# RWKV-7 mixing: the next group's last inverse product, scores and transpose between the state steps, and other places for the projected block's finish, the group norm's first parts and the result copies

## The chip, the cores and the metric

The kernel runs on one core of a Trainium2 chip. Its time is the device time of one execution, in microseconds (us), and the number that stands for a kernel is the median of its runs. The kernel before has 1464.78 us, the median of three runs from 1461.38 to 1465.36.

A core has a matrix engine (TensorE, PE in the profile), a vector engine (VectorE, DVE), an activation engine (ScalarE, ACT), a general engine (GpSimd, POOL) and a queue engine that issues transfers (SyncE, SP). Each of them works through its own list of instructions in order and waits for another engine only where an instruction says so.

## The reference, cut to what matters

One decoder layer on 1024 positions: a projection `w_in`, three mixers beside each other (HGRN2, windowed attention, RWKV-7), an output projection, a gated MLP and a gated embedding. The change lies in the RWKV-7 mixer, with four heads of width 64. For each head it computes a recurrence over the positions, and a norm of every position's result over its 64 values:

```python
def step(state, inp):
    r_t, w_t, k_t, v_t, kk_t, a_t = inp
    sa = jnp.einsum('bhvk,bhk->bhv', state, -kk_t)
    state = (state * w_t[:, :, None, :] + sa[..., None] * (kk_t * a_t)[:, :, None, :]
             + v_t[..., None] * k_t[:, :, None, :])
    return state, jnp.einsum('bhvk,bhk->bhv', state, r_t)
...
_, y = lax.scan(step, s0, xs)
y = y.swapaxes(0, 1)
mean = jnp.mean(y, axis=-1, keepdims=True)
var = jnp.mean((y - mean) ** 2, axis=-1, keepdims=True)
y = ((y - mean) * lax.rsqrt(var + RK_GN_EPS)).reshape(B_, S_, RK_WIDTH) * ln_w + ln_b
```

Other columns of `w_in` feed the other two mixers. Their products are independent of the recurrence, and the kernel uses them as filling work.

## The kernel before, in words

**The recurrence in chunks.** The four heads are taken as two pairs, p = 0 and p = 1, one pair after the other; a pair fills the 128 partitions. The 1024 positions are cut into 16 chunks of 64. Inside a chunk the recurrence becomes a triangular system, whose inverse is prepared as two tables, T and U, of 32-wide blocks. Only the state S goes from chunk to chunk.

**Groups.** `rwkv_groups` takes four chunks at a time, so a pair has four groups, g = 0 to 3. In the profiled execution the groups of p 0 lie at about 146 to 216 us, those of p 1 at about 334 to 404 us. A group does the following, in this order:

- finish of an earlier projected block and parts of the norm, in some groups (below);
- the *turn* of v: two transposes on TensorE (L821), then a filling block;
- py (L860), the last product of the inverse, whose copy into SBUF on ScalarE is Y (L861), and on GpSimd the next group's score table ABt (`scores_bd`, L801);
- *place* copies on ScalarE (L828): v into XV, and after the turn of ar, ar into xr;
- the scores sc (L871), of which VectorE takes the masked AKt and W (L785), a filling block, and pu (L882) from Y and U, which VectorE copies into U (L883);
- the turn of bhat, copied by VectorE into pb (L828), then on VectorE the next group's T under its mask (`quad("T")`, L794), and on GpSimd W from pb (L888);
- the turn of khat, placed by ScalarE into W; a filling block; pk, copied by ScalarE into xr (L897); two filling blocks;
- px (L901), of which ScalarE takes half of X (L903) and XV (L905) and VectorE the other half of X (L903); two filling blocks;
- pgm (L909), to which VectorE adds the addend and writes GM (L913), and pn (L922), from which VectorE makes N; the split of a projection weight (`pending("w")`) and a filling block;
- four *state steps*, u = 0 to 3: a product pS of GM and S (L939), from which VectorE makes the next S with one instruction (L940), and the products of the result pyo (L942, L944). A filling block follows the step u = 0;
- on VectorE the next group's U under its mask (`quad("U")`, L794), on ScalarE the four copies of the result from pyo into the pair's output (L954).

The first step of group 0 needs no product, since the state before it is zero.

**Filling blocks.** `fill(1)` issues one step of a projection that is independent of the recurrence: three products of 512 columns (L130, L132, L134) into the block dp. Three projected blocks, 48 steps, are spread over a pair. A weight of a projected block is split in two parts before use: ScalarE casts (L106), GpSimd subtracts (L108). When a block is complete, `pending("z")` issues its *finish* at the next place where it is called: in p 0 two multiplies on VectorE (L470); in p 1, for the block that is complete in group 1, twice a multiply (L306), a sigmoid on ScalarE (L473) and a second multiply (L475). A store on SyncE follows.

**The norm.** The first half of a pair's result, groups 0 and 1, is normed while groups 2 and 3 run, in four parts: part 0 takes the mean off (L727 to L729, VectorE), part 1 squares (L732, ScalarE), part 2 makes the variance (L735, L736, VectorE, and a power on GpSimd), part 3 multiplies (L740, VectorE).

**What sets the order.** The groups are issued inside `manual_schedule` for TensorE, VectorE, ScalarE and GpSimd: these engines get their instructions in the order in which the code is written. SyncE's order is the scheduler's. The products' results go to a pool of four PSUM buffers, tag `mx` (py, pt, sc, pu, pk, px, pgm, pn, pyo and pS).

## Time and profile before

| | kernel before |
|---|---|
| median of three runs | 1464.78 us (1461.38 to 1465.36) |
| profiled execution | 1464.15 us |
| its span, from the first to the last instruction | 1462.4 us |
| mean granted TensorE clock | 0.994 |
| busy, of the span: PE, DVE, ACT, POOL | 98%, 75%, 44%, 31% |

All rows of the profile come from the one profiled execution. A row of the order of time has the start in us, the duration in us, the engine, the line and the operation, written as output<-inputs with the tile shapes; a bracket at the end gives the idle time before the instruction and what ended it. `x8` means that eight instructions stand in one row. A row of a table of stretches has the bounds of the stretch, its length, then for PE, weight loads, DVE, ACT and POOL the busy time with the number of instructions, and at the end the granted TensorE clock, the share of the DMA engines and GB/s.

### The profile page before, as it was taken

The page shows a single profiled execution, that of the slowest core. Times are in us where ns is not written, and L with a number is a line of the kernel's source. Part 1 is how long each engine was busy: PE and PEld are TensorE (multiplying, and loading weights), DVE is VectorE, ACT ScalarE, POOL GpSimd, SP SyncE. Part 2 cuts the span into 40 slices and gives each one's busy share as a digit, 9 for nine tenths or more (in the row PEclk, how much of TensorE's full clock was granted, in tenths as well). Part 3 has the DMA queues.
Part 4 walks back from the last instruction along what each step waited for, and adds up shares of the span by engine and source line. Part 5 has one row for each costly group of instructions (what it writes and reads, how often), then busy time and mean ns, then how long its engine had stood idle before and what let it go on. Part 6 is the DMA issues. An engine that isn't in the chain of part 4 may idle for free.

```text
span 1462.4 us, 20341 instructions
## 1 busy us (share of the span) xinstructions
PE 1431.1 (98%) x7480; PEld 1178.0 (81%) x7480; DVE 1099.2 (75%) x1672; ACT 636.1 (44%) x1131; POOL 447.8 (31%) x364
## 2 busy tenths in 40 slices
PE   9999999999999999899989999999999999999996
PEld 7888887888877777788878888888888888888885
DVE  7667565674677688638778898888898799777685
ACT  6531443213434565335544344444444444455552
POOL 3331342223321131222144554444554000002342
PEclk9999999999999999999999999999999999999998
DMA  6123021240251320265423333333233883352343
GB/s 220 63 90 105 33 71 58 65 130 30 73 188 51 108 73 30 71 219 204 156 87 105 99 100 108 102 108 106 97 107 111 309 293 95 102 172 58 123 157 116
DMA packets 80020, 167.84 MB, mean 115 GB/s; under 512 B 20081, under 2 KB 22257, under 8 KB 79921
## 3 DMA queue, kind: packets, MB, share of 16 engines
q1 hardware_dynamic: 65568, 145.44, 30.2%
q10 hardware_dynamic: 13408, 17.57, 3.6%
q0 software_dynamic: 944, 3.54, 0.7%
q8 instruction: 59, 0.97, 0.3%
q14 instruction: 41, 0.33, 0.1%
HBM read 120.12 MB, written 46.40 MB: 114 GB/s over the span
## 4 chain that ended last, share of the span: by engine, by line
PE 87%; DVE 4%; issue 3%; ACT 2%; POOL 2%; DMA 2%; SPq 0%; DVEq 0%; ACTq 0%; POOLq 0%
PE bg L1351 16%; PE bv L1351 12%; PE dp L130 8%; PE dp L134 8%; PE dp L132 8%; PE bg L1652 7%; PE bv L1652 7%; PE hsc L1029 1%; PE bv L130 1%; PE bv L132 1%; PE bv L134 1%; PE bg L130 1%; PE bg L134 1%; PE bg L132 1%; PE swq L1186 1%
## 5 line engine op out<-in xcount | busy, mean ns | idle before, releaser
L130 PE MATMUL dp<-xh,whi 128*128 128x512 f32 x544 | 197.5, 408 | 0.8 <-ACT xh L375 0.8
L134 PE MATMUL dp<-xh,wlo 128*128 128x512 f32 x544 | 188.9, 392 | 0.3 <-POOL wlo L108 0.3
L132 PE MATMUL dp<-xl,whi 128*128 128x512 f32 x544 | 188.6, 392 | 0.0
L108 POOL TENSOR_TENSOR wlo<-raw,whi 128x512 fp32r<-128x512 f32 x84 | 138.0, 1662 | 80.9 <-ACT whi L106 80.9
L108 POOL TENSOR_TENSOR wlo<-wraw,whi 128x512 fp32r<-128x512 f32 x63 | 89.2, 1420 | 226.2 <-ACT whi L106 208.2
L1351 PE MATMUL bg<-t,whi 128*128 128x512 f32 x352 | 132.7, 389 | 0.0
L106 ACT CAST whi<-wraw 128x512 fp32r<-128x512 f32 x120 | 72.6, 617 | 129.1 <-PE dp L132 87.1
L130 PEld LDWEIGHTS dp<-xh,whi 128*128 128x128 f32 x544 | 101.6, 189 | 23.6 <-issue 3.5
L134 PEld LDWEIGHTS dp<-xh,wlo 128*128 128x128 f32 x544 | 102.3, 188 | 22.5 <-POOL wlo L108 0.7
L132 PEld LDWEIGHTS dp<-xl,whi 128*128 128x128 f32 x544 | 102.5, 189 | 20.2 <-DVE xl L376 0.5
L108 POOL TENSOR_TENSOR wlo<-s,whi 128x512 fp32r<-128x512 f32 x44 | 65.7, 1492 | 159.1 <-ACT whi L106 159.1
L106 ACT CAST whi<-raw 128x512 fp32r<-128x512 f32 x88 | 52.6, 619 | 100.3 <-PE bv L1351 51.5
L1652 PE MATMUL bg<-t,whi 128*128 128x512 f32 x308 | 94.9, 389 | 0.0
L1652 PE MATMUL bv<-t,whi 128*128 128x512 f32 x308 | 94.8, 389 | 0.0
L106 ACT CAST whi<-s 128x512 fp32r<-128x512 f32 x66 | 38.9, 620 | 120.7 <-PE bg L1351 113.0
L175 POOL TENSOR_TENSOR rst<-rst,mhalf 128x4 f32<-128x4 f32 (+1 forms) x9 | 10.2, 1130 | 222.7 <-DVE rst L173 222.7
L108 DVE TENSOR_TENSOR wlo<-wraw,whi 128x512 fp32r<-128x512 f32 x57 | 47.7, 837 | 40.2 <-ACT whi L106 35.8
L1351 PEld LDWEIGHTS bg<-t,whi 128*128 128x128 f32 x352 | 66.1, 188 | 13.7
L1648 ACT CAST t<-t 128x512 fp32r<-128x512 f32 x77 | 47.8, 622 | 47.9 <-PE bv L1652 33.0
L1652 PEld LDWEIGHTS bv<-t,whi 128*128 128x128 f32 x308 | 57.8, 188 | 12.0
L1652 PEld LDWEIGHTS bg<-t,whi 128*128 128x128 f32 x308 | 57.8, 188 | 11.9
L1351 PE MATMUL bg<-t,wlo 128*128 128x512 f32 x176 | 67.2, 389 | 0.0
(424 smaller groups left out, 3616.6 us busy)
## 6 DMA issues: line engine op xcount, KB each, us to landing
raw<-in_ffn_up_dram SPq DMA_DIRECT2D x44, 512.0 KB, 3.7
wraw<-in_w_in_dram SPq DMA_DIRECT2D x29, 512.0 KB, 3.7
z<-zst SPq DMA_DIRECT2D x18, 512.0 KB, 3.0
gb<-ct SPq DMA_DIRECT2D x33, 256.0 KB, 2.3
t<-gb SPq DMA_DIRECT2D x33, 256.0 KB, 2.8
t<-gt SPq DMA_DIRECT2D x33, 256.0 KB, 2.7
zl<-z SPq DMA_DIRECT2D x16, 512.0 KB, 4.5
wraw<-in_ple_gate_dram SPq DMA_DIRECT2D x16, 512.0 KB, 3.6
```

Of the source, the lines that this page charges most:

```text
L106: nc.scalar.copy(hi, src)
L108: eng.tensor_tensor(lo, src, hi.bitcast(F32), ALU.subtract)
L130: nc.tensor.matmul(ps[hf], wh, xh[hf], start=first, stop=False)
L132: nc.tensor.matmul(ps[hf], wh, xl[hf], start=False, stop=False)
L134: nc.tensor.matmul(ps[hf], wl, xh[hf], start=False, stop=last)
L175: nc.gpsimd.tensor_tensor(r2[:, :n], r[:, :n], self.mhalf[:, :n], ALU.pow)
L1029: nc.tensor.matmul(sc[:, c, :], ks[:, c * P:(c + 1) * P], view(qt, c * P, [2 * n, 64 // n], [HT + n, 2], [1, n]), start=True, stop=True)
L1186: nc.tensor.matmul(pq[h][:, b:b + w], d["q"][hs, qb * P:nk], d["k"][hs, b:b + w], start=True, stop=True)
L1351: nc.tensor.matmul(ps, w[part == 2][:, s], X[k][part == 1], start=start and k == part == 0, stop=k == 3 and part == 2, skip_group_check=no ...
L1648: nc.scalar.copy(xh, x)
L1652: nc.tensor.matmul(ps[m], wt[part == 2][:, m * P:(m + 1) * P], (xh, xl)[part == 1], start=k == part == 0, stop=k == NK - 1 and part == 2)
```

## The change

Only `rwkv_groups` is changed; no product, copy or transfer is added or left out.

- py, its copy Y, the next group's score table and the next group's U under its mask are issued in the state steps, after the step u = 1 (`inverse_first`, then `quad("U")`). For group 0, whose U is made ahead of the loop as before, py stands ahead of the loop.
- The next group's turn of v and its filling block are issued after the step u = 2 (`values_turn`, `fill(1)`). In the last group, where nothing comes next, a filling block and norm part 3 stand after u = 1.
- The four result copies of a group are issued in the next group, after the place copies of v and ar (`result`); those of the last group behind the loop.
- `pending("z")` and, in group 2, norm part 0 move from the head of the group to behind the place of khat.
- Norm part 1 moves in group 2 from behind the place of ar to behind the copies of px; norm part 2 moves from group 2 to group 3, at the same place in the group.

There are 37 filling blocks in the groups instead of 36, and one less behind them.

```diff
+        def inverse_first(g):
+            t["Y"] = rt("Y", [P, 4, P])
+            py = mxp.tile([P, 4, P], F32, tag="mx", name=self.nm("py"))
+            for u in range(4):
+                nc.tensor.matmul(py[:, u, :], t["AB", g][:, u, :], t["T", g][:, u, :], start=True, stop=True)
+            nc.scalar.copy(t["Y"], py)
+            if g < 3:
+                scores_bd(g + 1)
+
+        def values_turn(g):
+            t["pv"] = turn(lambda b: v[:, 256 * g + P * b:256 * g + P * b + P])
+
+        def result(g, py):
...
+                    nc.scalar.copy(y4[64 * c:64 * c + 64, 2 * g:2 * g + 2, h, :], py4[64 * h:64 * h + 64, :, c, :])
+
+        S, before = None, None
+        values_turn(0)
+        fill(1)
+        inverse_first(0)
         for g in range(4):
...
-            Xr = rt("xr", [P, 4, P])
-            self.pending("z")
-            if g == 2:
-                self.rwkv_norm_in(p, d, 0, (0,))
-            if last:
-                self.rwkv_norm_in(p, d, 0, (3,))
-            pv = turn(lambda b: v[:, t2(b)])
-            fill(1)
-            Y = rt("Y", [P, 4, P])
-            py = mxp.tile([P, 4, P], F32, tag="mx", name=self.nm("py"))
...
-            place(pv, lambda h: XV[:, :, h, :], nc.scalar.copy, 1)
+            Xr, Y = rt("xr", [P, 4, P]), t["Y"]
+            place(t["pv"], lambda h: XV[:, :, h, :], nc.scalar.copy, 1)
             place(turn(lambda b: ar[:, c2(b), 0, :].rearrange("p c i -> p (c i)")), lambda h: Xr[:, :, 0:64], nc.scalar.copy)
-            if g == 2:
-                self.rwkv_norm_in(p, d, 0, (1,))
+            if before:
+                result(*before)
...
-            if g == 2:
+            if g == 3:
                 self.rwkv_norm_in(p, d, 0, (2,))
             place(turn(lambda b: d["kh"][:, t2(b)]), lambda h: W[:, :, h, 1, :], nc.scalar.copy, 1)
+            self.pending("z")
+            if g == 2:
+                self.rwkv_norm_in(p, d, 0, (0,))
             fill(1)
...
                 nc.scalar.copy(XV[q, :, h, :], px[q, :, 64:128])
+            if g == 2:
+                self.rwkv_norm_in(p, d, 0, (1,))
             fill(2)
...
                 if u == 0:
                     fill(1)
-            if not last:
-                quad("U", g + 1)
...
+                if u == 1:
+                    if last:
+                        self.rwkv_norm_in(p, d, 0, (3,))
+                        fill(1)
+                    else:
+                        inverse_first(g + 1)
+                        quad("U", g + 1)
+                if u == 2 and not last:
+                    values_turn(g + 1)
+                    fill(1)
+            before = g, py
+        result(*before)
```

**TensorE, p 1, from the end of group 1's state steps into group 2**, in the kernel before (pS and pyo are the state steps, pt a turn, dp a filling block):

```order
L939 MATMUL pS_3208<-S_3200,GM_2864 128x64
L942 MATMUL pyo_3189<-XV_2866,W_2865 64x64 x2
L944 MATMUL pyo_3189<-S_3200,GM_2864 128x64
L939 MATMUL pS_3215<-S_3207,GM_2864 128x64
L942 MATMUL pyo_3189<-XV_2866,W_2865 64x64 x2
L944 MATMUL pyo_3189<-S_3207,GM_2864 128x64
L821 MATMUL pt_3242<-cst,v_2304 128x128 x2
L130 MATMUL dp_3183<-xh_107,whi_3015 128x512
L132 MATMUL dp_3183<-xl_108,whi_3015 128x512
L134 MATMUL dp_3183<-xh_107,wlo_3017 128x512
L860 MATMUL py_3249<-T_3115,ABt_3075 128x128 x4
L821 MATMUL pt_3261<-cst,ar_2043 128x128 x2
```

The same place in the changed kernel, where L939 is L953, L942 and L944 are L956 and L958, and L860 is L849:

```order
L849 MATMUL py_3208<-T_3115,ABt_3048 128x128 x4
L953 MATMUL pS_3219<-S_3200,GM_2864 128x64
L956 MATMUL pyo_3189<-XV_2866,W_2865 64x64 x2
L958 MATMUL pyo_3189<-S_3200,GM_2864 128x64
L821 MATMUL pt_3225<-cst,v_2304 128x128 x2
L130 MATMUL dp_3183<-xh_107,whi_3015 128x512
L132 MATMUL dp_3183<-xl_108,whi_3015 128x512
L134 MATMUL dp_3183<-xh_107,wlo_3017 128x512
L953 MATMUL pS_3232<-S_3218,GM_2864 128x64
L956 MATMUL pyo_3189<-XV_2866,W_2865 64x64 x2
L958 MATMUL pyo_3189<-S_3218,GM_2864 128x64
L821 MATMUL pt_3243<-cst,ar_2043 128x128 x2
```

py now stands ahead of the third state product, the turn of v and the filling block ahead of the fourth, and the turn of ar follows directly behind the last step.

**ScalarE, p 1, group 2**, in the kernel before, from the result copies of group 1 (sc<-pyo) to the copy of pk into xr (zst is the projected block's finish, oc norm part 1):

```order
L954 COPY sc_2307<-pyo_3189 64x2x64 x4
L473 ACTIVATE zst_3228<-dp_2894 128x512 x2
L861 COPY Y_3248<-py_3249 128x512
L828 COPY XV_2866<-pt_3242 64x2x64 x4
L828 COPY xr_3227<-pt_3261 64x2x64 x4
L732 ACTIVATE oc_3237<-sc_2307 128x512
L828 COPY W_2865<-pt_3305 64x2x64 x4
L897 COPY xr_3227<-pk_3315 128x4x64
```

The same place in the changed kernel, where L861 is L850, L954 is L862, L897 is L909, L903 is L915 and L905 is L917:

```order
L850 COPY Y_3207<-py_3208 128x512
L828 COPY XV_2866<-pt_3225 64x2x64 x4
L828 COPY xr_3238<-pt_3243 64x2x64 x4
L862 COPY sc_2307<-pyo_3189 64x2x64 x4
L828 COPY W_2865<-pt_3285 64x2x64 x4
L473 ACTIVATE zst_3292<-dp_2893 128x512 x2
L909 COPY xr_3238<-pk_3309 128x4x64
L915 COPY X_2863<-px_3325 64x4x64
L917 COPY XV_2866<-px_3325 64x4x64 x2
L732 ACTIVATE oc_3301<-sc_2307 128x512
```

Y is now the first of the group's copies, the result copies stand behind the place of ar, and the two sigmoids stand between the place of khat and the copy of pk.

**VectorE, p 1, group 2**, in the kernel before, from U's mask to the copy of half of X:

```order
L794 TENSOR_TENSOR U_3221<-Tc_2510,cst 128x512
L306 TENSOR_TENSOR dp_2894<-dp_2894,rstd 128x512
L475 TENSOR_TENSOR zst_3228<-zst_3228,dp_2894 128x512
L306 TENSOR_TENSOR dp_2894<-dp_2894,rstd 128x512
L475 TENSOR_TENSOR zst_3228<-zst_3228,dp_2894 128x512
L727 TENSOR_REDUCE gnm_3238<-sc_2307 128x8
L728 TENSOR_SCALAR gnm_3238<-gnm_3238 128x8
L729 TENSOR_TENSOR sc_2307<-sc_2307,gnm_3238 128x512
L785 TENSOR_TENSOR AKt_3276<-sc_3269,pm_2858 128x256
L785 TENSOR_TENSOR W_2865<-sc_3269,pm_2858 64x4x64 x2
L883 COPY_PREDICATED U_3221<-cmask,pu_3283 128x512
L828 COPY pb_2862<-pt_3289 64x2x64 x4
```

The same engine in the changed kernel, from the masked AKt on (L883 is L892):

```order
L785 TENSOR_TENSOR AKt_3261<-sc_3254,pm_2858 128x256
L785 TENSOR_TENSOR W_2865<-sc_3254,pm_2858 64x4x64 x2
L892 COPY_PREDICATED U_3216<-cmask,pu_3268 128x512
L828 COPY pb_2862<-pt_3274 64x2x64 x4
L794 TENSOR_TENSOR T_3281<-Tc_2503,cst 128x512
L306 TENSOR_TENSOR dp_2893<-dp_2893,rstd 128x512
L475 TENSOR_TENSOR zst_3292<-zst_3292,dp_2893 128x512
L306 TENSOR_TENSOR dp_2893<-dp_2893,rstd 128x512
L475 TENSOR_TENSOR zst_3292<-zst_3292,dp_2893 128x512
L727 TENSOR_REDUCE gnm_3302<-sc_2307 128x8
L728 TENSOR_SCALAR gnm_3302<-gnm_3302 128x8
L729 TENSOR_TENSOR sc_2307<-sc_2307,gnm_3302 128x512
```

The seven instructions L306 to L729, which stood ahead of AKt, now stand behind T's mask, and the next instruction behind them is the copy of px into X (L915).

More of the change, by code (lines that the diff above doesn't have):

```diff
@@ L843, in rwkv_groups @@
         add_ar(0)
-        S = None
+        def inverse_first(g):
[9 more added lines that the diff above has]
+        def result(g, py):
+            y4 = y3.rearrange("p (b h) v -> p b h v", h=2)
+            py4 = py.rearrange("p (b two) v -> p b two v", two=2)
+            for h in (0, 1):
+                for c in (0, 1):
+                    nc.scalar.copy(y4[64 * c:64 * c + 64, 2 * g:2 * g + 2, h, :], py4[64 * h:64 * h + 64, :, c, :])
[3 more added lines that the diff above has]
+        inverse_first(0)
         for g in range(4):
@@ L848, in rwkv_groups @@
             t2 = lambda b: slice(256 * g + P * b, 256 * g + P * b + P)
-            Xr = rt("xr", [P, 4, P])
-            self.pending("z")
-            if g == 2:
-                self.rwkv_norm_in(p, d, 0, (0,))
-            if last:
-                self.rwkv_norm_in(p, d, 0, (3,))
-            pv = turn(lambda b: v[:, t2(b)])
-            fill(1)
-            Y = rt("Y", [P, 4, P])
-            py = mxp.tile([P, 4, P], F32, tag="mx", name=self.nm("py"))
-            for u in range(4):
-                nc.tensor.matmul(py[:, u, :], t["AB", g][:, u, :], t["T", g][:, u, :], start=True, stop=True)
-            nc.scalar.copy(Y, py)
-            if not last:
-                scores_bd(g + 1)
-            place(pv, lambda h: XV[:, :, h, :], nc.scalar.copy, 1)
+            Xr, Y = rt("xr", [P, 4, P]), t["Y"]
+            place(t["pv"], lambda h: XV[:, :, h, :], nc.scalar.copy, 1)
             place(turn(lambda b: ar[:, c2(b), 0, :].rearrange("p c i -> p (c i)")), lambda h: Xr[:, :, 0:64], nc.scalar.copy)
-            if g == 2:
-                self.rwkv_norm_in(p, d, 0, (1,))
+            if before:
+                result(*before)
             ps = mxp.tile([P, 4, 2, 64], F32, tag="mx", name=self.nm("sc"))
@@ L947, in rwkv_groups @@
                     fill(1)
-            if not last:
-                quad("U", g + 1)
-            y4 = y3.rearrange("p (b h) v -> p b h v", h=2)
-            py4 = py.rearrange("p (b two) v -> p b two v", two=2)
-            for h in (0, 1):
-                for c in (0, 1):
-                    nc.scalar.copy(y4[64 * c:64 * c + 64, 2 * g:2 * g + 2, h, :], py4[64 * h:64 * h + 64, :, c, :])
+                if u == 1:
[10 more added lines that the diff above has]
+        result(*before)
     def hgrn_setup(self):
```

## The prediction

> **What bounds the kernel now.** I read the page's first part and its chain of waits, then the stretches of single groups, then the order of time on TensorE, VectorE and ScalarE there.
>
> ```profile
> PE 1431.1 (98%) x7480; PEld 1178.0 (81%) x7480; DVE 1099.2 (75%) x1672; ACT 636.1 (44%) x1131; POOL 447.8 (31%) x364
> PE 87%; DVE 4%; issue 3%; ACT 2%; POOL 2%; DMA 2%; SPq 0%; DVEq 0%; ACTq 0%; POOLq 0%
> ```
>
> TensorE sets the end, and the change adds and removes no product. So it can only win time in which TensorE stands, and lose where TensorE is made to stand. The stretches below are p 1's groups 1 and 2, each from one turn of v to the next; p is the pair of heads, g the group.
>
> ```profile
> 351.08:367.92 16.84, 16.80 (x141) 14.31 (x141) 8.03 (x21) 6.23 (x21) 5.59 (x9) 1.00 0.10 32
> 367.92:386.62 18.70, 17.27 (x141) 14.26 (x141) 13.22 (x29) 10.12 (x28) 9.90 (x12) 1.00 0.07 29
> ```
>
> Group 1 is a clean group; group 2 takes 18.70 - 16.84 = 1.86 us more with the same 141 products. TensorE in time, group 1 and the first waits of group 2:
>
> ```profile
> 353.12 1.06 PE L871 MATMUL sc<-ar,kbd 128*128 128x128 f32 x8
> 355.61 0.38 PE L821 MATMUL pt<-cst,bhat 128*128 128x128 f32 x2
> 356.03 0.44 PE L821 MATMUL pt<-cst,khat 128*128 128x128 f32 x2
> 359.20 1.05 PE L901 MATMUL px<-xr,U 128*128 128x128 f32 x8
> 361.47 1.05 PE L909 MATMUL pgm<-pb,X 128*128 128x128 f32 x8
> 365.42 0.33 PE L939 MATMUL pS<-S,GM 128*128 128x64 f32 x2
> 366.21 0.39 PE L939 MATMUL pS<-S,GM 128*128 128x64 f32 x2
> 367.07 0.39 PE L939 MATMUL pS<-S,GM 128*128 128x64 f32 x2
> 367.92 0.39 PE L821 MATMUL pt<-cst,v 128*128 128x128 f32 x2
> 368.85 1.05 PE L860 MATMUL py<-T,ABt 128*128 128x128 f32 x8
> 372.49 1.16 PE L882 MATMUL pu<-U,Y 128*128 128x128 f32 x8 [0.77 <-ACT Y L861]
> 374.73 0.44 PE L821 MATMUL pt<-cst,khat 128*128 128x128 f32 x2 [0.66 <-ACT xr L828]
> ```
>
> The reader is to see three losses. In group 2, pu waits for Y and the turn of khat for ScalarE's place copies. In every group khat starts 0.42 after bhat, where its followers need about 0.2: a hidden wait of 0.20. And the chained state products lie 0.86 and 0.85 apart where the first step takes 0.79: 0.13 a group.
>
> **The change part by part.** *State steps.* The product py (L860), the turn of v and a filling block now stand between the state products, so S is ready when its product comes. I take back 0.13 in p 0's and p 1's groups 1 and 2, and 0.21 in groups 0, where three steps of 0.86 follow each other: 4 x 0.13 + 2 x 0.21 = 0.94. What a py after a state step costs beside one after a filling block no row shows; I take nothing, with 0.07 (0.86 less 0.79) either way at six places, 0.4.
>
> *Copies before khat.* Y is now copied during the state steps, so after the last step ScalarE begins with the place copies of v and ar, and stores the group's result only then.
>
> ```profile
> 368.18 1.08 ACT L954 COPY sc<-pyo 64x128 f32<-64x128 f32 x4 [6.21 <-PE pyo L944]
> 371.36 0.60 ACT L473 ACTIVATE zst<-dp 128x512 f32<-128x512 f32 x1 [1.49 <-DVE dp L306]
> 371.86 0.58 ACT L861 COPY Y<-py 128x512 f32<-128x512 f32 x1
> 372.46 1.11 ACT L828 COPY XV<-pt 64x128 f32<-64x128 f32 x4
> 373.60 1.07 ACT L828 COPY xr<-pt 64x128 f32<-64x128 f32 x4
> 376.52 0.37 ACT L897 COPY xr<-pk 128x256 f32<-128x256 f32 x1
> ```
>
> The result copy began 0.26 after the last state product (368.18 - 367.92). The score products (sc) now begin one turn, 0.22, after that step, so the v copies start at sc + 0.04, and ar is copied at 0.04 + 1.14 + 1.10 (373.60 - 372.46 = 1.14) = sc + 2.28. khat comes at sc + 2.7 (355.61 - 353.12 + 0.22): no wait. That gives 0.20 in each of groups 1 to 3 of both p, 6 x 0.20 = 1.20, and takes away the 1.86 of p 1's group 2. All gains: 0.94 + 1.20 + 1.86 = 4.00 us. The first groups' order is not changed.
>
> *Group 2: where the finish and the norm go.* The finish of the projected block (L306, L473, L475, twice) and the first norm part (L727 to L729) leave the head of group 2 and stand behind the T product mask.
>
> ```profile
> 357.67 0.69 DVE L794 TENSOR_TENSOR T<-Tc,cst 128x512 f32<-128x512 f32 x1
> 360.75 0.43 DVE L903 COPY X<-px 64x256 f32<-64x256 f32 x1 [2.39 <-ACT X L903]
> 369.91 0.69 DVE L475 TENSOR_TENSOR zst<-zst,dp 128x512 f32<-128x512 f32 x1 [0.92 <-ACT zst L473]
> 370.63 0.70 DVE L306 TENSOR_TENSOR dp<-dp,rstd 128x512 f32<-128x512 f32 x1
> 372.60 0.68 DVE L727 TENSOR_REDUCE gnm<-sc 128x8 f32<-128x512 f32 x1
> 373.31 0.17 DVE L728 TENSOR_SCALAR gnm<-gnm 128x8 f32<-128x8 f32 x1
> 373.52 0.69 DVE L729 TENSOR_TENSOR sc<-sc,gnm 128x512 f32<-128x512 f32 x1
> 374.13 0.42 DVE L785 TENSOR_TENSOR AKt<-sc,pm 128x256 f32<-128x256 f32 x1
> ```
>
> In p 1, ScalarE's two sigmoids now stand ahead of the copy of pk into xr (L897), and px (L901) needs xr. A pass of 0.69 lets the next start after 0.61 (374.13 - 373.52), so VectorE is free behind T at sc + 4.55 + 0.61 = 5.16. From there: L306 until the sigmoid starts 0.73 (371.36 - 370.63), sigmoid and handover 0.63, L475 until L306 0.72, to the second sigmoid 0.73, until ScalarE's next copy 0.50 (371.86 - 371.36), that copy 0.37, to TensorE 0.06 (373.60 + 1.07 to 374.73): 3.74, so px starts at sc + 8.90. It is due at 359.20 - 353.12 - 0.20 = sc + 5.88. **TensorE stands 3.02.** The X copy comes behind the second L475, L727, L728 and L729 at 5.16 + 3.44 + 0.61 + 0.71 + 0.21 + 0.61 = 10.74, is ready 0.43 + 0.06 later at 11.23, and pgm is due at px + 2.27 (361.47 - 359.20) = 11.17: 0.06. Together 3.08.
>
> In p 0 the finish has no sigmoid, only two multiplies (their 1.20 from the next fence): 5.16 + 1.20 + 0.71 + 0.21 + 0.61 = 7.89, X ready at 8.38; pgm is due at 5.88 + 2.27 = 8.15: 0.23.
>
> *Group 3.* The result copy (1.10 with its gap) now lies ahead of the weight cast that VectorE waits for, and the second norm part (L735, L736) ahead of the next finish and of X.
>
> ```profile
> 391.55 0.62 ACT L106 CAST whi<-wraw 128x512 fp32r<-128x512 f32 x1
> 393.42 1.20 DVE L828 COPY pb<-pt 64x128 f32<-64x128 f32 x4
> 394.94 1.29 DVE L470 TENSOR_TENSOR zst<-dp,rstd 128x512 f32<-128x512 f32 x2 [0.32 <-PE dp L134]
> ```
>
> The cast starts at sc + 2.28 + 1.10 + 0.01 = 3.39, the pb copies 1.87 after it as here (393.42 - 391.55) at 5.26, and take 1.23; the reduce 0.71, L736 0.21, the multiplies 1.20, X 0.43, the way 0.06: 9.10 against 8.15 due, so 0.95. In p 0 a sigmoid lies between ScalarE's copies of X and XV; for what it holds up I take 0.3, an estimate of half of L473's 0.60, with 0 and 0.6 as ends: 1.25. Losses: 3.08 + 0.23 + 0.95 + 1.25 = 5.51; against 4.00 that is **1.5 us slower**. Nothing else is paid: U's mask (L794) stands now between two state results, with a py of 0.89 and a v turn with its filling block of 0.93 (368.85 - 367.92) to cover its 0.69; the projected block's store on SyncE goes 5 us later and SyncE's order stays.
>
> *What a standing TensorE costs behind it.* The granted clock halves after a sparse stretch:
>
> ```profile
> 491.72:495.13 3.41, 1.63 (x13) 1.10 (x12) 1.88 (x6) 3.40 (x8) 0.00 (x0) 1.00 0.92 345
> 495.13:498.54 3.41, 3.41 (x19) 3.41 (x18) 0.09 (x1) 0.82 (x3) 0.00 (x0) 0.50 0.84 330
> 611.19:614.60 3.41, 1.87 (x13) 1.36 (x12) 1.44 (x4) 0.00 (x0) 1.01 (x1) 1.00 0.00 0
> 614.60:618.01 3.41, 3.37 (x17) 2.26 (x15) 2.61 (x3) 1.24 (x2) 1.29 (x1) 1.00 0.27 76
> ```
>
> A stretch of 3.41 with 1.78 idle is followed by one at 0.50, one with 1.54 idle by full clock. These stretches lie on a grid, since 611.19 is 35 steps of 3.413 after 491.72. A stand of 3.0 leaves more than 1.78 in one such stretch unless the grid cuts it between 1.2 and 1.8, so the drop comes in about 1 - 0.6/3.41, 0.8 of executions. It costs half of 3.41, 1.7, less what falls into the stand itself: I take 1.4, with 0 and 1.7 as ends. The Trainium skill (TensorE: Matmul & The Clock Gate, HAM oscillation — how this bites in real kernels) gives the rule "no PE-idle gaps >~3.4µs", by which a stand of 3.0 keeps the clock and the sum stays at 1.5; the rows, where about half a stretch idle was enough, decide.
>
> **Rivals.** *A: slower by more.* POOL's large passes stretch VectorE where a stretch now counts:
>
> ```profile
> 182.36 1.09 DVE L728 TENSOR_SCALAR gnm<-gnm 128x8 f32<-128x8 f32 x1
> 387.05 1.57 DVE L794 TENSOR_TENSOR U<-Tc,cst 128x512 f32<-128x512 f32 x1
> 383.89 4.18 POOL L108 TENSOR_TENSOR wlo<-wraw,whi 128x512 fp32r<-128x512 f32 x3
> ```
>
> L728 took 1.09 instead of 0.17, U's mask 1.57 instead of 0.69 beside three POOL passes. In group 2 of p 1, U's mask and a weight split now both stand before the third state result, beside the same three passes. The product that needs this result is due 0.79 + 0.89 + 0.79 + 0.93 = 3.40 after the second step's; two chained steps would take 1.72 of that, of which VectorE works some 0.6, so about 2.3 are free, and two passes of 1.57 take 0.8 too much. With L728's 0.92 in p 0: 1.5 + 1.4 + 1.7 = 4.6 slower, 1469.4. It decides once both passes exceed 1.15 each. Against it: in p 0, POOL stands idle behind its W copies when L728 now comes. The Trainium skill (SBUF — State Buffer, SBUF: two separate sides) has VectorE with two SBUF inputs and a reading GpSimd exclude each other for whole instructions; the 1.57 row agrees.
>
> *B: no halved clock.* 1464.78 + 1.5 = 1466.3; for it, the stretch at 611.19 kept the clock behind it; against it, only 1.54 of that was idle.
>
> *C: the move does what it says.* The sigmoid chain and the late X cost no more than before: gains of 4.00 against 3.08, or 1463.9. For it: VectorE idled 2.39 ahead of X in group 1. Against it: 3.4 of chain do not fit into 2.39, and ScalarE takes its queue in order.
>
> **How the numbers follow.** The profiled execution took 1464.15 (span 1462.4 and 1.75 around it), the median of three runs is 1464.78, 0.63 above. 1.5 + 1.4 = 2.9 gives 1467.1 on the profiled one and **1467.7** for the median. Chances: the forecast 0.46, A 0.20, B 0.21, C 0.13. The range: from C less 0.9 for the 0.4 of handovers and the spread of the runs, 1463.0, to A with the full 1.7 for the clock and 1.3 of the same, 1471.0; the likeliest's own is 1466.0 to 1469.5. Within 0.3%, 4.4 us, is about what this measurement cannot tell from no change: A passes it, and the forecast's upper end sometimes. Slower 0.22; faster 0.03, since all gains together are 4.0; same 0.75.
>
> **What would show it.** In the profile after: khat 0.22 behind bhat and state products no longer chained (gains); px of p 1's group 2 with an idle of about 3 us, released by ScalarE's copy into xr (the main loss); the granted clock at 0.5 within 4 us of it (1.4); pgm late by about 1 us in both groups 3. Wrong if px of that group starts within 1 us of its due time, if pgm is on time in group 3, or if the clock stays at 1.00 behind a stand of 3 us.

## The result and the profile after

The changed kernel takes 1465.92 us (median of 19 runs, 1462.62 to 1468.47), the kernel before 1462.70 us (median of 19, 1459.73 to 1465.36). The ratio is 1.0023 with a 95% interval of 1.0015 to 1.0030: 3.2 us slower, between 2.2 and 4.4. The profiled execution took 1464.79 us with a span of 1463.0. The three runs shown first for the kernel before had a median of 1464.78, so they lay 2.1 above the median of 19. That is why the forecast of 1467.7 stands 1.8 above the measured time, while the difference that it rests on, 2.9, is near the measured 3.2.

The busy times of the page, which answer to the first line shown of before:

```profile
PE 1430.1 (98%) x7480; PEld 1175.7 (80%) x7480; DVE 1098.4 (75%) x1672; ACT 635.3 (43%) x1131; POOL 449.7 (31%) x364
```

Nothing moves there: the work is the same, and what changed is where TensorE stands. The groups show it. The stretches run from the scores product of one group to that of the next (columns as before: bounds, length, busy time of PE, weight loads, DVE, ACT, POOL, granted clock, DMA). First the kernel before, p 0's group 2 and p 1's groups 1 and 2:

```profile
182.12:199.20 17.08, 17.00 (x142) 14.39 (x140) 13.06 (x27) 9.03 (x26) 12.16 (x12) 1.00 0.13 45
353.12:369.96 16.84, 16.80 (x142) 14.31 (x140) 8.57 (x22) 6.83 (x22) 5.56 (x8) 1.00 0.06 22
369.96:388.66 18.70, 17.27 (x142) 14.26 (x140) 14.14 (x30) 9.52 (x27) 11.35 (x12) 1.00 0.13 46
```

The same three in the changed kernel:

```profile
182.22:199.63 17.41, 17.07 (x142) 14.12 (x140) 12.58 (x26) 8.98 (x27) 8.93 (x10) 1.00 0.13 41
353.89:370.52 16.63, 16.63 (x141) 14.27 (x140) 7.91 (x20) 6.21 (x22) 5.61 (x8) 1.00 0.08 29
370.52:393.45 22.93, 20.02 (x141) 16.60 (x140) 14.08 (x28) 10.05 (x29) 8.93 (x10) 0.85 0.09 33
```

A clean group gains 0.21 (16.84 to 16.63), p 1's group 2 loses 4.23, p 0's group 2 loses 0.33. TensorE in time, from the end of p 1's group 1 to the end of group 2:

```profile
366.02 0.33 PE L953 MATMUL pS<-S,GM 128*128 128x64 f32 x2
366.82 1.11 PE L849 MATMUL py<-T,ABt 128*128 128x128 f32 x8
367.77 0.33 PE L953 MATMUL pS<-S,GM 128*128 128x64 f32 x2
368.57 0.39 PE L821 MATMUL pt<-cst,v 128*128 128x128 f32 x2
370.52 1.06 PE L880 MATMUL sc<-ar,kbd 128*128 128x128 f32 x8
373.01 0.38 PE L821 MATMUL pt<-cst,bhat 128*128 128x128 f32 x2
373.25 0.44 PE L821 MATMUL pt<-cst,khat 128*128 128x128 f32 x2
379.50 2.08 PE L913 MATMUL px<-xr,U 128*128 128x128 f32 x8 [2.91 <-ACT xr L909]
383.93 1.91 PE L923 MATMUL pgm<-pb,X 128*128 128x128 f32 x8
391.29 0.39 PE L821 MATMUL pt<-cst,v 128*128 128x128 f32 x2
392.35 0.41 PE L953 MATMUL pS<-S,GM 128*128 128x64 f32 x2
```

khat follows bhat after 0.24 instead of 0.42, and in group 2 without the wait of 1.86. Then px stands 2.91 us for ScalarE's copy into xr, and behind it px takes 2.08 instead of 1.05, pgm comes 4.43 after px instead of 2.27. ScalarE in the same place:

```profile
376.50 0.60 ACT L473 ACTIVATE zst<-dp 128x512 f32<-128x512 f32 x1 [1.70 <-DVE dp L306]
378.58 0.60 ACT L473 ACTIVATE zst<-dp 128x512 f32<-128x512 f32 x1 [1.49 <-DVE dp L306]
379.08 0.37 ACT L909 COPY xr<-pk 128x256 f32<-128x256 f32 x1
393.06 0.82 ACT L828 COPY XV<-pt 64x128 f32<-64x128 f32 x3 [1.08 <-PE pyo L956]
396.09 0.62 ACT L106 CAST whi<-wraw 128x512 fp32r<-128x512 f32 x1
```

The copy into xr, 0.37 us of work, waits in ScalarE's queue behind two sigmoids, which wait for VectorE (the last two rows belong to group 3 and are used below). And the clock, in stretches of 3.413 us around it:

```profile
375.47:378.88 3.41, 1.12 (x5) 0.56 (x3) 2.37 (x4) 0.89 (x2) 0.76 (x1) 1.00 0.00 0
378.88:382.29 3.41, 2.79 (x11) 2.60 (x12) 2.37 (x5) 0.94 (x3) 0.00 (x0) 0.50 0.37 154
382.29:385.71 3.42, 3.42 (x13) 2.87 (x11) 0.20 (x1) 3.13 (x7) 0.00 (x0) 0.50 0.00 0
```

TensorE idles 2.29 of the first stretch; the next two are at half clock, 6.83 us in all. Less the 0.62 in which TensorE stood anyway, that costs (6.83 - 0.62) / 2 = 3.1 us in this execution.

Behind the groups the two profiled executions come together again. The second turn for the norm of p 1 (L752) starts at 417.87, against 412.83 before, 5.04 later. Counted from p 0's first scores (148.66 and 148.28) it is 269.21 us against 264.55, 4.66 later: 3.1 of the clock and 1.6 of waits. The spans end only 0.6 apart. The kernel before lost clock at two later places in its profiled execution, at 495 (quoted in the prediction) and at 748; the changed kernel did at neither, since there the grid cut the same stands otherwise. The 1.78 us idle ahead of 495, for one, fall in the changed kernel into two stretches, 0.69 (from 494.94) and 1.09 (from 498.35). The one at 748, first before, then after the change:

```profile
744.31:747.73 3.42, 1.30 (x6) 1.08 (x7) 2.66 (x3) 0.00 (x0) 0.91 (x1) 1.00 0.40 149
747.73:751.14 3.41, 3.41 (x10) 2.63 (x9) 0.00 (x0) 0.22 (x1) 0.00 (x0) 0.50 0.00 0
```

```profile
747.52:750.93 3.41, 1.82 (x9) 1.50 (x9) 2.59 (x4) 0.18 (x1) 1.81 (x1) 1.00 0.50 159
```

So one pair of profiled executions would mislead by some 4 us, and only the groups' stretches in the traces and the medians over many executions are to be compared. The executions of the changed kernel show the clock's part in their times: the five with a mean clock of 0.992 took 1465.5 to 1468.5 us, the five with 0.995 or 0.996 took 1462.6 to 1464.8.

### The profile page after: what moved, and what is told of

It is laid out like the page before. It is cut to its first block, busy times and chain, and to the rows that moved or that the text cites. A ratio compares the mean times of both kernels' runs of the same rounds, so it can differ in the third digit from the quotient of the medians.

```text
span 1463.0 us, 20342 instructions
## 1 busy us (share of the span) xinstructions
PE 1430.1 (98%) x7480; PEld 1175.7 (80%) x7480; DVE 1098.4 (75%) x1672; ACT 635.3 (43%) x1131; POOL 449.7 (31%) x364
## 4 chain that ended last, share of the span: by engine, by line
PE 85%; DVE 5%; issue 3%; ACT 2%; POOL 2%; DMA 2%; SPq 0%; DVEq 0%; ACTq 0%; POOLq 0%
PE bg L1370 16%; PE bv L1370 12%; PE dp L130 8%; PE dp L134 7%; PE dp L132 7%; PE bg L1671 7%; PE bv L1671 7%; PE hsc L1048 1%; PE bv L130 1%; PE bv L132 1%; PE bv L134 1%; PE bg L130 1%; PE bg L132 1%; PE bg L134 1%; PE swq L1205 1%
```

## The experiments

My theory: the loss lies in the finish with its sigmoids, in one block ahead of xr and X, and in the clock that halves behind that stand; the new order of the state steps gains a little. The rivals: the state steps' order is the loss; VectorE's work ahead of X is the whole loss, whatever stands on ScalarE; ScalarE's queue is the whole loss, whatever stands on VectorE; the clock has another cause. Each ratio is to the kernel before, run beside it on the same chip.

### The finish and the norm alone at their new places

In the kernel before:

```diff
             Xr = rt("xr", [P, 4, P])
-            self.pending("z")
-            if g == 2:
-                self.rwkv_norm_in(p, d, 0, (0,))
...
             place(turn(lambda b: d["kh"][:, t2(b)]), lambda h: W[:, :, h, 1, :], nc.scalar.copy, 1)
+            self.pending("z")
+            if g == 2:
+                self.rwkv_norm_in(p, d, 0, (0,))
             fill(1)
```

The norm's parts 1 to 3 move to the changed kernel's places as well, and with part 3 a filling block.

> The kernel before with the finish of the projected block and the norm's parts at the changed kernel's places; py, the turn of v, U's mask and the result copies stay where they were. If the finish ahead of the copy of pk is the loss (my theory): the wait of 1.86 us at khat in p 1's group 2 goes, px of that group stands about 3.0 us for ScalarE's copy into xr, the clock halves behind it (2.4 us on the mean of several executions, 0 to 3.4 in one), X is late by 0.5 us in p 0's group 2 and by 0.3 in both groups 3: about 4.7 us slower than before, 0.2% to 0.4%. If the order of the state steps is the loss (rival): no slower than before, since a wait of 1.86 us is gone.

Measured: 1467.12 us (8 runs) against 1462.98, ratio 1.0031 (1.0018 to 1.0044), 4.5 us slower. px:

```profile
380.45 1.16 PE L897 MATMUL px<-xr,U 128*128 128x128 f32 x8 [2.74 <-ACT xr L893]
```

The stand is there without the new step order, and its clock halves for one stretch from 381.5. So the loss comes with the finish and the norm part behind it, not with the order of the state steps; the next runs take the two apart.

### The state steps alone in their new order

In the changed kernel:

```diff
             Xr, Y = rt("xr", [P, 4, P]), t["Y"]
+            self.pending("z")
+            if g == 2:
+                self.rwkv_norm_in(p, d, 0, (0,))
             place(t["pv"], lambda h: XV[:, :, h, :], nc.scalar.copy, 1)
...
-            if before:
-                result(*before)
...
-            before = g, py
-        result(*before)
+            result(g, py)
```

The calls at the place of khat go, and the norm's parts 1 to 3 go back as well.

> The changed kernel with result copies, finish and all norm parts back at the places that they had before; only py, Y, the scores, U's mask and the turn of v stay between the state steps. If the result copies had to make room (my theory): ScalarE now has 1.1 us of result copies ahead of the place copies, so khat waits about 0.5 us in groups 1 and 3 of both p and about 3.0 in p 1's group 2, where the sigmoids come ahead too, with a halved clock behind that: 3 to 6 us slower than before, 0.2% to 0.4%. If the step order gains by itself (rival): khat waits no more than before, and it is 1 to 3 us faster than before.

Measured: 1466.71 us (7 runs) against 1462.81, ratio 1.0027 (1.0016 to 1.0038), 3.9 us slower. The turns of p 1's groups 1 and 2:

```profile
358.63 0.44 PE L821 MATMUL pt<-cst,khat 128*128 128x128 f32 x2 [0.53 <-ACT xr L828]
377.52 0.44 PE L821 MATMUL pt<-cst,bhat 128*128 128x128 f32 x2 [2.35 <-ACT XV L828]
378.62 0.69 PE L821 MATMUL pt<-cst,khat 128*128 128x128 f32 x2 [0.66 <-ACT xr L828]
```

0.53 in a group without a finish, 2.35 + 0.66 = 3.0 in the group with one, as expected. So neither half of the change gains alone: the new step order needs the result copies out of the way, and the finish needs a place where nobody waits for it.

### The finish without its sigmoids

For the block that ends in p 1's group 2 the sigmoids and second multiplies are left out, so its values are not the reference's.

```diff
     def finish(self, kind, dst, src, r):
+        if self.plain:
+            kind = 2
         if kind == 2:
             self.nc.vector.tensor_tensor(dst, src, r, ALU.mult)
...
+            self.plain = p == 1 and g == 2
             self.pending("z")
+            self.plain = False
```

> The changed kernel, with the finish of the block that ends in p 1's group 2 reduced to two multiplies, as in p 0: its sigmoids and second multiplies are left out, so that block's values are not the reference's. If the chain through ScalarE is the loss (my theory): px of that group is on time, pgm late by 0.3 to 0.5 us as in p 0, no halved clock there: 5.5 us less than the changed kernel on the profile, 1 to 3 us faster than before, 0.1% to 0.2%. If VectorE's work ahead of X is the loss (rival): pgm is late by about 3 us instead, and the time stays within 1.5 us of the changed kernel, 0.1% to 0.3% slower than before.

Measured: 1461.44 us (12 runs) against 1462.98, ratio 0.9993 (0.9982 to 1.0003): 1.0 us below before, at the lower end of the 1 to 3 expected and not told from no change by the interval, and 4 to 5 below the changed kernel. From p 0's first scores to the second turn for the norm of p 1 its execution takes 263.70 us (148.68 to 412.38) against 269.21, 5.5 less, as expected. px has no wait, and pgm is late as in p 0:

```profile
379.22 1.13 PE L929 MATMUL pgm<-pb,X 128*128 128x128 f32 x8 [0.33 <-DVE X L921]
```

The chain through ScalarE is what made px stand; VectorE's other passes ahead of X cost 0.5.

### The finish one place further on, behind the copy of pk

```diff
             place(turn(lambda b: d["kh"][:, t2(b)]), lambda h: W[:, :, h, 1, :], nc.scalar.copy, 1)
-            self.pending("z")
-            if g == 2:
-                self.rwkv_norm_in(p, d, 0, (0,))
             fill(1)
...
             nc.scalar.copy(Xr[:, :, 64:128], pk)
+            self.pending("z")
+            if g == 2:
+                self.rwkv_norm_in(p, d, 0, (0,))
             fill(2)
```

> The changed kernel with the finish and norm part 0 one place further on, behind ScalarE's copy of pk into xr. My theory: px of p 1's group 2 is then on time, but VectorE still has its seven passes ahead of X, so pgm waits about 3.1 us for X instead: the same stand one product later, the same time as the changed kernel within 1 us, 0.1% to 0.3% slower than before. If ScalarE's queue order alone is the cause (rival), the stand goes, and it is 5 us less than the changed kernel, about 2 faster than before.

Measured: 1467.14 us (6 runs) against 1462.81, ratio 1.0031 (1.0018 to 1.0044).

```profile
382.41 1.42 PE L923 MATMUL pgm<-pb,X 128*128 128x128 f32 x8 [3.17 <-DVE X L915]
```

px is on time, 3.17 behind khat (373.64 to 376.81), and pgm stands 3.17 for X: the same stand one product later. To free ScalarE's queue is not enough; the copy of X stands behind the same chain on VectorE.

### And norm part 0 behind the copies of X

```diff
             for h, q in enumerate(Q):
                 nc.scalar.copy(XV[q, :, h, :], px[q, :, 64:128])
             if g == 2:
-                self.rwkv_norm_in(p, d, 0, (1,))
+                self.rwkv_norm_in(p, d, 0, (0, 1))
```

> As the one before (finish behind the copy of pk), with norm part 0 moved on behind the copies of X. My theory: X comes behind the last second multiply, 1.6 us late in p 1's group 2 and on time in p 0's; the stand of 1.6 leaves the clock in most executions, and norm part 0 makes GM late by up to 0.6: 3 us less than the changed kernel, between 0.1% faster and 0.1% slower than before. If the order behind px does not matter (rival), as the run before: 0.1% to 0.3% slower than before.

Measured: 1463.53 us (11 runs) against 1462.81, ratio 1.0004 (0.9991 to 1.0017): no change, 3 us below the changed kernel.

```profile
380.45 1.13 PE L921 MATMUL pgm<-pb,X 128*128 128x128 f32 x8 [1.65 <-DVE X L913]
```

```profile
377.92:381.34 3.42, 1.77 (x12) 1.30 (x11) 2.62 (x6) 1.58 (x4) 0.00 (x0) 1.00 0.20 81
381.34:384.75 3.41, 3.41 (x35) 2.60 (x33) 2.91 (x7) 2.70 (x5) 2.11 (x4) 1.00 0.18 74
```

The stand of 1.65 lies whole in one stretch, and the clock stays at 1.00 behind it.

### Idle products in the stand

```diff
             fill(2)
+            if p == 1 and g == 2:
+                idle = mxp.tile([P, 4, P], F32, tag="mx", name=self.nm("idle"))
+                for u in range(12):
+                    nc.tensor.matmul(idle[:, u % 4, :], self.ident, self.ident, start=True, stop=True)
             px = mxp.tile([P, 4, P], F32, tag="mx", name=self.nm("px"))
```

> The changed kernel with twelve more products of 128 columns, of a constant with itself and read by nobody, ahead of px in p 1's group 2: 2.7 us of work put into the stand. If the stand halves the clock behind it (my theory): px starts at the same time as in the changed kernel within 0.3 us, the clock stays at 1.00, and the time is about 2.4 us less than the changed kernel's (0 to 3.4 by execution), 0.5 to 1.5 us slower than before, although the kernel does more work. If the clock has another cause (rival): the clock halves at the same place, and the time is that of the changed kernel, 3.2 us slower than before, or more.

Measured: 1468.71 us (6 runs) against 1462.98, ratio 1.0049 (1.0032 to 1.0065), 7 us slower: a miss for the time. At the place itself the expectation holds:

```profile
376.63 2.84 PE L914 MATMUL idle<-cst 128*128 128x128 f32 x24
379.71 1.16 PE L917 MATMUL px<-xr,U 128*128 128x128 f32 x8 [0.24 <-ACT xr L909]
```

```profile
379.41:382.82 3.41, 3.17 (x20) 2.55 (x20) 2.57 (x5) 1.27 (x4) 0.00 (x0) 1.00 0.38 154
```

px starts 0.21 later than in the changed kernel, as all of this execution does, the clock stays at 1.00, and group 2 takes 20.26 instead of 22.93. So the stand did halve the clock. Up to the second turn for the norm this execution takes 266.10 us from p 0's first scores (148.82 to 414.92), 3.1 less than the changed kernel. What the time lost lies elsewhere: the twelve products made the scheduler order some later instructions anew, in parts of the program whose order is not written by hand (VectorE's list differs from the changed kernel's in some 60 places behind the groups, ScalarE's in some 30). One place where it shows is a wait of TensorE of 1.61 us at 1383.6 for VectorE's L201, where the same row of the kernel before shows no idle time. How much of the 7 us each such place costs was not separated. In all other runs here the instructions behind the groups stand in the changed kernel's order, so their times can be compared.

### Useful blocks in the stand

```diff
-            fill(2)
+            fill(6 if p == 1 and g == 2 else 2)
             px = mxp.tile([P, 4, P], F32, tag="mx", name=self.nm("px"))
```

> The changed kernel with four more filling blocks ahead of px in p 1's group 2, taken from the end of the pair: 2.8 us of work that is due anyway put into the stand. By my theory the stand at px goes to under 0.5 us with px at the same time after pk, the clock stays at 1.00, and four blocks are left less behind the groups: 2.8 + 2.4 = 5.2 us less than the changed kernel, about 2 us faster than before, 0.05% to 0.25%. The rival: the next projected block is wanted four blocks earlier than its split weight is there, so the same 3 us stand at a filling block in group 3, and the time is that of the changed kernel or 2 us less at most.

Measured: 1464.69 us (12 runs) against 1462.98, ratio 1.0016 (1.0006 to 1.0027), 2.4 us slower, where 2 faster was expected, and where the rival had put it, though not for the rival's reason. px waits 0.19 and the clock holds; no filling block waits for its weight. But the four blocks are missing behind the groups, where they had covered the second half's norm. TensorE there, in this run:

```profile
415.02 1.12 PE L752 MATMUL yt<-cst,sc 128*128 128x128 f32 x4 [2.37 <-DVE sc L740]
```

```profile
411.56:414.98 3.42, 1.09 (x5) 0.56 (x3) 2.28 (x3) 0.62 (x1) 2.85 (x2) 1.00 0.68 274
414.98:418.39 3.41, 3.37 (x8) 2.25 (x9) 3.13 (x4) 0.00 (x0) 0.48 (x1) 0.50 0.82 243
```

The stand has moved: 2.37 us for the last norm part, and a halved clock behind it. Filling work is not free to take: it was cover for another chain.

### A version with the finish in pieces

In the changed kernel, the finish becomes four stages: A a multiply and a sigmoid, B the other multiply, C the other sigmoid, D the second multiplies and the store (for a block without sigmoids, A and B have its two multiplies). Norm part 0 is cut into a part 4, the mean, and a part 5, the subtraction.

```diff
             if before:
                 result(*before)
+            stage("C")
...
             place(turn(lambda b: d["kh"][:, t2(b)]), lambda h: W[:, :, h, 1, :], nc.scalar.copy, 1)
-            self.pending("z")
-            if g == 2:
-                self.rwkv_norm_in(p, d, 0, (0,))
+            stage("D")
+            if g == 3:
+                self.rwkv_norm_in(p, d, 0, (1,))
...
                 nc.scalar.copy(XV[q, :, h, :], px[q, :, 64:128])
-            if g == 2:
-                self.rwkv_norm_in(p, d, 0, (1,))
+            if g == 3:
+                self.rwkv_norm_in(p, d, 0, (2,))
...
                 if u == 2 and not last:
+                    if g < 2:
+                        stage("A")
+                    else:
+                        self.rwkv_norm_in(p, d, 0, (4,))
                     values_turn(g + 1)
                     fill(1)
+                if u == 3 and not last:
+                    if g < 2:
+                        stage("B")
+                    else:
+                        self.rwkv_norm_in(p, d, 0, (5,))
```

> The changed kernel with the finish cut in pieces: first multiply and first sigmoid behind the state result of u = 2, the next multiply behind that of u = 3, the second sigmoid behind the result copies, the last two multiplies behind T's mask; norm part 0 in two pieces behind the state results of u = 2 and u = 3 of group 2, part 1 behind the place of khat in group 3, part 2 behind the copies of px there. If the finish and the norm in one block ahead of X and xr are the whole loss (my theory), px and pgm of both groups 2 are on time (16.6 us from scores to scores, against 18.70 and 17.08 before and 22.93 and 17.41 in the changed kernel), pgm of groups 3 within 0.2 of its time, and the gains of the step order remain: 3 us faster than before, 0.05% to 0.35%. If VectorE has no room left in the state steps (rival), the state products come late by 0.5 us or more in groups 1 and 2 and the time is that of before or more.

Measured: 1459.05 us (10 runs) against 1462.81, ratio 0.9978 (0.9969 to 0.9987), 3.2 us faster than before by the ratio, and 0.45% below the changed kernel by the two ratios. p 1's groups 1 and 2:

```profile
353.38:370.01 16.63, 16.63 (x142) 14.27 (x141) 8.89 (x22) 6.81 (x23) 5.62 (x8) 1.00 0.07 28
370.01:386.85 16.84, 16.84 (x142) 14.14 (x140) 12.30 (x27) 8.98 (x27) 8.94 (x10) 1.00 0.13 46
```

The waits of TensorE at khat, px and pgm are gone in the two groups. Group 2 still takes 0.21 more than group 1, where 16.6 was expected for both. It is lost at the state product behind the turn of v, which comes 1.08 after it (384.67 to 385.75) instead of 0.93, behind VectorE's mask of U (1.04) and weight split (1.75).

### The pieces without the new step order, and the pieces again

In the kernel before, with the stages of the run above (C behind the place of ar) and its norm parts:

```diff
-            self.pending("z")
-            if g == 2:
-                self.rwkv_norm_in(p, d, 0, (0,))
-            if last:
-                self.rwkv_norm_in(p, d, 0, (3,))
             pv = turn(lambda b: v[:, t2(b)])
...
             place(turn(lambda b: ar[:, c2(b), 0, :].rearrange("p c i -> p (c i)")), lambda h: Xr[:, :, 0:64], nc.scalar.copy)
-            if g == 2:
-                self.rwkv_norm_in(p, d, 0, (1,))
+            stage("C")
...
                 if u == 0:
                     fill(1)
+                if u == 1 and last:
+                    self.rwkv_norm_in(p, d, 0, (3,))
+                if u == 2 and not last:
+                    if g < 2:
+                        stage("A")
+                    else:
+                        self.rwkv_norm_in(p, d, 0, (4,))
```

> The kernel before, with the finish cut in pieces and the norm's parts placed as in the run with pieces; py, the turn of v, U's mask and the result copies stay at their old places, and the second sigmoid stands behind the place copies of v and ar. My theory: the wait of 1.86 us in p 1's group 2 and the 0.24 that p 0's group 2 takes over a clean group go (16.84 from scores to scores in both, as in groups 1), while khat still stands 0.42 behind bhat: 2.1 us faster than before, 0% to 0.25%; the order of the state steps then is worth the 1.1 us by which the changed kernel with pieces is below this one. The rival, that the pieces gain only together with the new step order: group 2 of p 1 stays above 18 us, and the time is that of before within 1 us.

> The changed kernel with the finish in pieces once more, beside the run before it, to compare the two on one chip: by my theory 1.1 us below that run on the profiles' groups (16.6 to 16.85 us from scores to scores in groups 1 and 2, khat 0.22 to 0.25 behind bhat), and 3 us faster than the kernel before, 0.1% to 0.35%. By the rival (the step order gains nothing by itself) both times agree within what the runs tell apart, and the groups' stretches too.

Measured on one chip: 1462.23 us (12 runs) for the pieces alone, ratio 0.9989 (0.9979 to 0.9999), and 1459.77 us (12 runs) with the new step order, ratio 0.9981 (0.9972 to 0.9989), both against 1462.56. In the pieces alone p 1's group 2 is a clean one:

```profile
370.46:387.28 16.82, 16.78 (x141) 14.30 (x140) 11.35 (x25) 9.00 (x26) 9.74 (x11) 1.00 0.15 51
```

p 0's group 2 stays at 17.09, a miss of 0.25. The expectation put this excess down to the norm. The trace has a weight split there, which stands on VectorE between two state results and takes 1.04, and the state product behind it comes 1.06 after the one before it (195.51 to 196.57) instead of 0.86:

```profile
195.28 1.04 DVE L108 TENSOR_TENSOR wlo<-wraw,whi 128x512 fp32r<-128x512 f32 x1
196.57 0.43 PE L979 MATMUL pS<-S,GM 128*128 128x64 f32 x2
```

The kernel before has the same at this place, a split of 1.03 and a product 1.05 after the one before it (195.21 to 196.26), so its group 2 of p 0 took 17.08.

By the ratios, cutting the finish is worth some 1.6 us and the new order another 1.2, which agrees with the 1.1 expected. The two intervals overlap, and by the medians it is 0.3 and 2.5, so the runs alone do not split the sum of some 2.8. The traces do: from p 0's first scores to the second turn for the norm of p 1 it is 264.55 us in the kernel before, 262.85 (148.60 to 411.45) with the pieces alone and 261.65 (148.36 to 410.01) with the new order, all at full clock: 1.7 and 1.2.

## Why the prediction was right

The sign, the place and the size of the difference came out. By time alone, 1465.92 lies just under the 1466.0 to 1469.5 that the forecast gave itself, next to rival B's 1466.3; the difference to the kernel before and the clock's rows speak for the forecast. By its own terms, with what the traces show (rows above, and for p 0 and groups 3 the ones below):

| term | predicted | measured |
|---|---|---|
| state steps | -0.94 | -0.24 |
| khat, six groups | -1.20 | -1.08 |
| the wait in p 1's group 2 | -1.86 | -1.86 |
| px of p 1's group 2 | +3.02 | +3.08 |
| X in p 0's group 2 | +0.23 | +0.49 |
| X in groups 3 (p 1, p 0) | +0.95, +1.25 | +0.36, +0.30 |
| state product late, end of p 1's group 2 | 0, in rival A | +0.21 |
| sum without the clock | +1.5 | +1.3 |
| halved clock | +1.4 | +3.1 in this execution |

The sum came nearer than its terms. Groups 3 were put 1.54 too high, and the other terms of waits together 1.35 too low (state steps 0.70, khat 0.12, px 0.06, X in p 0 0.26, the late state product 0.21). That the two cancel to 0.2 is luck.

**The main loss** was right in mechanism and size: px was due 3.17 behind khat, at 376.42, and came at 379.50.

**State steps.** The step that failed is the 0.13 to 0.21 taken back at each boundary. Each step takes 0.80 to the next instruction now, but py behind a state step takes 0.95 (366.82 to 367.77) where it took 0.89 behind a filling block. From the second step's product to the scores it is 4.50 after (366.02 to 370.52) and 4.54 before (365.42 to 369.96): 0.04, six times. Most of the gain went into py, for which a bound of 0.07 had been left open.

**Groups 3** were oversized, and the sign named for them, pgm late by about 1 us in both, was missed: it is late by 0.36 and 0.30. The step had ScalarE's place copies start 0.04 behind the scores, so that the cast came at 3.39. In the trace the first XV copy runs a filling block earlier, and the other three start as soon as the last step's products have read XV, 0.39 ahead of the scores (393.06 against 393.45); the cast follows at 2.64. In p 0 no more than 0.30 of the expected 1.25 is left. The rows, TensorE in p 0's group 2 and p 1's group 3:

```profile
188.13 1.05 PE L913 MATMUL px<-xr,U 128*128 128x128 f32 x8
190.89 1.13 PE L923 MATMUL pgm<-pb,X 128*128 128x128 f32 x8 [0.34 <-DVE X L915]
399.30 1.05 PE L913 MATMUL px<-xr,U 128*128 128x128 f32 x8
401.93 1.16 PE L923 MATMUL pgm<-pb,X 128*128 128x128 f32 x8 [0.21 <-DVE X L915]
```

pgm was due 2.27 behind px, and came 2.76 and 2.63 behind it.

**X in p 0's group 2** was undersized by 0.26. VectorE, there and at the next group's U mask in p 1:

```profile
190.31 0.43 DVE L915 COPY X<-px 64x256 f32<-64x256 f32 x1
389.31 1.03 DVE L794 TENSOR_TENSOR U<-Tc,cst 128x512 f32<-128x512 f32 x1
390.26 1.75 DVE L108 TENSOR_TENSOR wlo<-wraw,whi 128x512 fp32r<-128x512 f32 x1
```

The working had X start 7.89 behind the scores, at 190.11. It started at 190.31: from T's mask to the first multiply and from norm part 0 to X it took 0.71 and 0.72, where the working had 0.61 for each.

**Rival A's mechanism** exists at a quarter of its price. U's mask took 1.03 and the weight split 1.75 beside POOL's passes, and the state product behind the turn of v came 1.06 after it instead of 0.93. From the second step's product to the scores it is 4.71 there (388.74 to 393.45) instead of 4.50: 0.21 in p 1, where 0.8 was worked out. In p 0 it is 4.71 too, but the kernel before took 4.78 (194.42 to 199.20), for the weight split that stood between its state results. Only one of the two passes was above the 1.15 from which it was to decide, and L728 in p 0, for which rival A had 0.92 more, took its 0.17. The Trainium skill (SBUF — State Buffer, SBUF: two separate sides) has the pair of ports held for a whole instruction; passes lengthened from 0.69 to 1.03 and 1.75 agree with a wait for part of a POOL pass, and no run here shows the lock itself.

**The clock** was right in kind and undersized in this execution: two halved stretches instead of one. Over the executions the median moved by 3.2, where 2.9 was forecast; less the 1.3 of the other terms that leaves some 1.9 for the clock, an estimate. The runs with the stand filled (clock 1.00) and with a stand of 1.65 (clock 1.00) agree with the rule that the prediction took from the rows. Rival B, no halved clock, falls for the same reason. Rival C fails as well: the chain did not fit into VectorE's idle time, and where the finish was put behind the copy of pk, it did not fit either.

## What to carry to other kernels

A chain that goes to and fro between two engines blocks both queues for its whole length, so it is moved as pieces into the gaps of each queue, not as a block: as a block behind one product it only moved the stand to the next. Before a block of filling work is moved into a stand, look for what it covers where it is now. Where a stand is left, it costs itself as long as no stretch of the clock's grid holds more than about half of it idle. Where one did, a halved stretch of some 1.7 us came on top, and in the profiled execution of the changed kernel two of them.

## What was not expected of the hardware

**The clock goes by about half a stretch, and a halved stretch can repeat.** On the grid of 3.413 us, behind the first 15 us and ahead of the last 20, the traces of all these kernels hold 17 stretches at full clock with 1.78 us idle or more; each is followed by one at 0.50. Of those with up to 1.69 us idle, none is. The one next below the limit, in the first run with the finish in pieces:

```profile
589.70:593.11 3.41, 1.72 (x20) 1.63 (x22) 2.10 (x4) 0.00 (x0) 0.00 (x0) 1.00 0.00 0
593.11:596.53 3.42, 3.42 (x44) 3.13 (x42) 2.24 (x5) 0.93 (x3) 0.01 (x1) 1.00 0.01 2
```

The limit so lies between 1.69 and 1.78 of 3.41, about half. In the last 20 us idle time does not decide: there, one stretch with 1.75 idle was followed by full clock, and in six runs one with only 1.06 to 1.52 by half. The changed kernel's, with 1.20 idle:

```profile
1450.67:1454.08 3.41, 2.21 (x16) 1.79 (x16) 1.42 (x6) 1.12 (x3) 1.39 (x2) 1.00 0.00 0
1454.08:1457.49 3.41, 0.15 (x2) 0.00 (x0) 3.41 (x10) 0.37 (x1) 2.77 (x4) 0.50 0.65 223
```

Eight of its sixteen products write a single column (L1783, 128x1), so its busy time may hold little work; this was not tested. Within the same bounds, a halved stretch in which TensorE idled no more than 0.10 was always followed by full clock; the one with 0.62 idle (378.88) by another at half. At half clock 2.79 busy us are the work of 1.4 at full clock, less than half a stretch, so a measure of work per stretch would explain this one too; it stays a guess. The Trainium skill (TensorE: Matmul & The Clock Gate, Part 1: The HAM clock gate (the "warmup" mystery)) has a free-running window of 3413 ns; the traces agree, with halved stretches of 3.41 and 6.83. By the rule of the same page of the Trainium skill (HAM oscillation — how this bites in real kernels), "no PE-idle gaps >~3.4µs", the stand of 3.1 us here would have kept the clock; it did not.

**The same kernel can lose clock at different places in each execution.** The two runs with the finish in pieces and the new order are one program: near 590 one stretch of the first holds 1.69 idle and the clock stays, one of the second holds 2.11 and the clock halves at 590.67. The stand near 745 halved the clock in the profiled executions of the kernel before, of the finish alone and of four others, and left it in the rest. At some 1.7 us for each such place, an estimate from half of 3.41, three of them would make up most of the 6 us by which executions of one kernel differ.
